# A hybrid attention and convolution layer step: first tiles, row sums, cache copies, turn and sample rows rearranged

## The chip, the cores and the metric

The kernel runs on one core of a Trainium2 chip. TensorE (PE in the rows, PEld for its weight loads) multiplies matrices, VectorE (DVE), ScalarE (ACT) and GpSimd (POOL) work on tiles, and SyncE (SP) issues every transfer into one queue that 16 DMA engines serve. The metric is the device time of one execution in microseconds (us). TensorE's clock is granted at one of two levels, 1.2 or 2.4 GHz; the profile shows the grant as a share, 0.5 or 1.0.

## What is computed

One layer for 512 prompt positions and 8 samples of 4 new tokens each, in fp32. The reference, cut:

```
h = rms_norm(x, norm_pre);  z = h @ w_in            # 2048 -> 60 column tiles of 128
q, k, v, g_att, c_a, c_b, g_conv = split(z)
att = attend(q, k, v)         # 12 heads; windows (128,1), (512,4), (2048,16), merged
u = c_a * sigmoid(c_b);  c = silu(layer_norm(depthwise_conv(u_pad)))
c = c @ conv_pw_w + conv_pw_b
mix = concat(att * silu(g_att), c * silu(g_conv))
y = mix @ w_out;  out = x + rms_norm(y, norm_post)
new_kv_sample = concat(cache_kv, k and v of the new tokens)[4:]   # per sample
```

The samples attend over a cache of 2048 rows of 12 KB for each of the 8 samples, and the last line is an output too: 2044 rows of each sample's cache come out again, moved up by four.

## The kernel before

Tokens are columns: 512 prompt tokens and 32 sample tokens, 544 in all, in two halves of 272. Products in fp32 are made of three fp32r matmuls: each operand is split into a rounded high part and the rest (`xh`, `xl` for x; `wh`, `wl` for weights; `mh`, `ml` and `owh`, `owl` in the output projection), and high*high, low*high and high*low are added in PSUM. ScalarE casts the high part, VectorE or GpSimd subtracts.

**First stage.** `project(n, ...)` makes one column tile of w_in: 16 rows of k, two halves, three matmuls, so 96 matmuls of 272 columns. The weights of a tile come in four loads of 256 KB (`load_w`, six buffers, five loads ahead) and are split on ScalarE (L800) and GpSimd (L801). For the first tile (n = 0) x itself arrives and is split (`split_x`, L250 and L251), and the sums of squares for the RMS norm are built along the way: a square of every x tile, and adds on VectorE and GpSimd (L257 to L261). `make_R` then turns the two partial sums into a factor for each token: ten pairs of matmuls `rqx`, a short chain on ScalarE and VectorE, diagonal tiles, matmuls `rbx`, and two copies into `R` (L302). No tile can leave PSUM before R is there. `make_tabs` (bias tables, matmuls `tb` and `rb`) runs in steps between the parts of tiles 1 and 2. From n = 3 on the samples' work runs beside the tiles.

**Order.** All engines' programs are held in the order in which the code is written (`in_order`). `tick()` counts quarter tiles; side jobs (heads, samples, convolution) are generators advanced at ticks. `bulk` copies cache rows from DRAM to DRAM whenever the bytes sent so far are under START + PACE * (columns that TensorE has been given): 8 MB + 159.5 bytes a column. `dma` issues all of it on SP, in order.

**Cache.** The samples' units (24 for K, 24 for V) load `kvf` (rows that are 16 apart, 0.75 MB, three buffers) and `kvm` (the last 512 rows, 1 MB, two buffers). What has been loaded is also written to the output from there (`store_far`, `store_mid`); the other rows go DRAM to DRAM, in 96 pieces of 1152 KB. In the V units the products `o` use four column groups of TensorE: four matmuls with 32 stationary columns each, one behind the other (`tile_position`, L106).

**Turn.** After tile 59, ScalarE and VectorE split all 16 tiles of the gated mix (`mh`, `ml`) and the samples' columns of them (`smix`), then the first w_out tiles. **Output projection.** Four column blocks c of 512; for each the row blocks (0, 1) and then (2, 3) of 128 tokens and the 32 sample rows, block 4. A step is one of 16 k rows: three matmuls of 512 columns for a prompt block, two for the samples (`smix` holds high and low side by side). In the last c the order is (0, 1), (2, 4), (3). `take_out` squares and scales, `finish` norms, adds x (`load_xt`) and stores.

Of the kernel before, what the change touches and what calls it, by code (L numbers as in the profile page):

```python
# [18 lines left out]
P = 128  # L19
D = 2048  # L20
# [17 lines left out]
TW = 640  # L38
PATTERNS = ((128, 1), (512, 4), (2048, 16))
# [5 lines left out]
START, PACE = 8_000_000, 159.5  # L45
# [37 lines left out]
def body(tc, xT, xtok, gpost, w_in, w_out, ckv, cconv, relb, vecs, pww, c_oht, c_ohr, c_lmr, c_tm, c_pick,  # L83
# [44 lines left out]
    last_w = [1 << 30]  # L128
# [16 lines left out]
    KORD = list(range(0, 8)) + list(range(12, 16)) + list(range(8, 12))  # L145

    def load_w(m):


        if m >= 4 * NTILE + NOUT or m in raws or m > last_w[0]:  # L150
            return
        n, qt = divmod(m, 4)
        raw = wpool.tile([P, 4, P], F32, tag="raw", name=f"raw{m}", bufs=6)
        if n < N_IN:
            dma(raw, w_in[order[n], qt])
        else:
            c, i = divmod(m - 4 * NTILE, KT)
            dma(raw.rearrange("p a b -> p (a b)"), w_out[c, KORD[i]])
        raws[m] = raw
# [25 lines left out]
    STARTS = (0, P, 2 * P, 3 * P, TOK - P)  # L185

    def token_rsqrt(sums, pool, name):


        ps = bank("q", f"rq{name}")  # L190
        for j, st in enumerate(STARTS):
            for i, ss in enumerate(sums):
                mm(ps[:, j:j + 1], ss[:, st:st + P], ones[:, 0:1], start=(i == 0), stop=(i == len(sums) - 1))
        r, v, w = [pool.tile([P, 5], F32, name=f"{n}{name}") for n in "rvw"]
        diag = pool.tile([P, 5, P], F32, name=f"diag{name}")
        nc.scalar.activation(r, ps[:, 0:5], AF.Sqrt, bias=epsc[:, 0:1], scale=1.0)
        nc.vector.tensor_scalar(v, ps[:, 0:5], EPS, None, op0=ALU.add)
# [4 lines left out]
        nc.vector.tensor_tensor(r, r, w, op=ALU.mult)  # L202
        out = []
        for hf, (j0, j1) in enumerate(((0, 3), (2, 5))):
            ps = bank("st"[hf], f"rb{name}{hf}")
            for j in range(j0, j1):
                if hf == 0 or j > 2:
                    nc.vector.tensor_scalar(diag[:, j, :], ident, r[:, j:j + 1], 2048.0, op0=ALU.mult, op1=ALU.mult)
                t0, t1 = max(j * P, hf * HT), min(j * P + P, hf * HT + HT)
                d0 = t0 - STARTS[j]  # L210
                mm(ps[:, t0 - hf * HT:t1 - hf * HT], ones, diag[:, j, d0:d0 + t1 - t0], start=True, stop=True)
            out.append(ps)
# [16 lines left out]
    rs_n = []  # L229
    ap_ = ExitStack()  # L230
# [4 lines left out]
    ssum = [ip.tile([P, TOK], F32, name=f"ssum{i}") for i in range(2)]  # L235

    def load_x(c):
        xr = ip.tile([P, 2, TOK], F32, tag="xr", name=f"xr{c}", bufs=6)
        dma(xr, xT[:, 2 * c:2 * c + 2, :])
# [4 lines left out]
    def split_x(c):  # L244
        xr = xrs.pop(c)
        for j in range(2):
# [8 lines left out]
            sq = ssum[k] if k < 2 else ip.tile([P, TOK], F32, tag="sq", name=f"sq{k}", bufs=3)  # L255
# [44 lines left out]
    def make_R():  # L300
        for hf, ps in enumerate(token_rsqrt(ssum, ip, "x")):
# [3 lines left out]
    d2d = [(b, a0, s0) for b in range(NB) for a0 in range(0, 96, 16) for s0 in (0, 6)]  # L305
    d2d_at = [0]

    def bulk(upto):
        while d2d_at[0] < len(d2d) and sent[0] < upto:
            b, a0, s0 = d2d[d2d_at[0]]  # L310
            d2d_at[0] += 1
            s = ckv[b].rearrange("(a s) c -> a (s c)", s=16)[a0:a0 + 16, (4 + s0) * ROW:(10 + s0) * ROW]
            o = o_kvs[b].rearrange("(a s) c -> a (s c)", s=16)[a0:a0 + 16, s0 * ROW:(6 + s0) * ROW]
# [3 lines left out]
    mixg = [keep.tile([P, 4, TOK], F32, name=f"mix{i}") for i in range(4)]  # L317
# [201 lines left out]
    def load_far(u):  # L519
# [4 lines left out]
        far = state["sp"].tile([P, 3, 512], F32, tag="kvf", name=f"kvf{u}", bufs=3)  # L524
# [13 lines left out]

    def store_far(u):
        g, kv, b = units[u]  # L540
        far = fars[u]
        off = (kv * NH + g * G4) * P
        dst = o_kvs[b, 0:NFAR, off:off + 512].rearrange("(a s) c -> a s c", s=16)
        dma(dst[15:31, 12:16, :], far[64:128, 0, :])
        dma(dst[0:15, 12:16, :], far[4:64, 0, :])
        dma(dst[31:63, 12:16, :], far[:, 1, :])
        dma(dst[63:95, 12:16, :], far[:, 2, :])

    def store_mid(u):
        g, kv, b = units[u]  # L550
        off = (kv * NH + g * G4) * P
        dma(o_kvs[b, NFAR - NT:PAST - NT, off:off + 512].rearrange("(j p) c -> p j c", j=4), mids[u])
# [17 lines left out]
    def k_phase(g, before):  # L570
# [53 lines left out]
        for b in range(NB):  # L624
# [10 lines left out]
            store_far(u)  # L635
# [12 lines left out]
            store_mid(u)  # L648
# [56 lines left out]
    def v_phase(g):  # L705
# [22 lines left out]
        for half in range(2):  # L728
            o = bank("acc", f"o{g}_{half}")
            for s in range(4):  # L730
# [5 lines left out]
                store_far(u)  # L736
# [3 lines left out]
                for j in range(8):  # L740
# [11 lines left out]
                    if j == 2:  # L752
# [5 lines left out]
                        store_mid(u)  # L758
# [24 lines left out]

    def add(gen, delay, rank):
# [4 lines left out]
    AHEAD = 5  # L789

    def split(ci):
        if ci >= 4 * NTILE or ci in splits:
            return
        for a in range(AHEAD + 1):
            load_w(ci + a)
        raw = raws.pop(ci)
        raws[ci] = None
# [396 lines left out]
```

## Time and profile before

| | |
|---|---|
| time, median of 3 runs | 1212.15 us (1211.03 to 1212.73) |
| the profiled execution | 1209.32 us, its span 1207.5 us |
| PE busy | 1158.5 us, 96% of the span |
| DVE, ACT, POOL busy | 686.3, 374.1, 419.9 us |
| DMA | 397.52 MB, the queue's packets fill 93.8% of 16 engines' span |
| mean granted clock | 0.98 |

How to read the rows below. A line of a stage table gives a stretch in us from the span's start, its length, then for PE, PEld, DVE, ACT and POOL the busy us with the number of instructions, the mean granted clock, the mean share of the 16 DMA engines that was busy and the GB/s that they moved. A line of the timeline gives start, length, engine, line of the code, operation, output and inputs, shape, and in brackets how long the engine had been idle and what ended that. In a row of PE, one fp32 matmul has two records; a fp32r matmul has one. PE spans are those of pipelined matmuls, so the rate is read from start to start. A DMA row gives the number of issues, the size and the median us from issue to landing.

### The profile page before, as it was taken

Reading aid. Unit: us, or ns where it says so; the run is one execution under the profiler, and the core shown is the slowest. Engines: PE = TensorE matmul, PEld = TensorE weight load, DVE = VectorE, ACT = ScalarE, POOL = GpSimd, SP = SyncE. Lnnn points to the kernel's source line nnn. Section 1 sums busy time; section 2 is a strip of 40 time slices with the busy share of each in tenths; the row PEclk is TensorE's granted clock in tenths of the full one; section 3 lists DMA queues with packets and bytes.
Section 4 is the critical chain, followed back from the end, with each engine's and each line's share of the span. In section 5 each row is a group of like instructions: output and inputs, shape, how many; then the busy total and the mean of one; then the engine's idle time right before and its main releaser. Section 6 shows DMA issues by size and latency. Waiting matters only on the chain.

```text
span 1207.5 us, 24127 instructions
## 1 busy us (share of the span) xinstructions
PE 1158.5 (96%) x9342; PEld 1063.2 (88%) x9342; DVE 686.3 (57%) x2015; ACT 374.1 (31%) x759; POOL 419.9 (35%) x357
## 2 busy tenths in 40 slices
PE   5899999999999999999999999999999959999995
PEld 4799999999899999999999999999999948888884
DVE  7306989789889988777332676982221161202125
ACT  6223333322122432331343333322212162214121
POOL 5244333343334332343233222433433442314120
PEclk8799999999999999999999999999999979999998
DMA  9599999999999999999999999989999949899997
GB/s 340 200 367 360 345 328 348 341 287 348 310 330 333 344 345 343 385 366 312 335 357 350 357 350 336 317 311 393 330 325 347 348 159 330 317 328 347 329 338 229
DMA packets 161255, 397.52 MB, mean 329 GB/s; under 512 B 20007, under 2 KB 22823, under 8 KB 157940
## 3 DMA queue, kind: packets, MB, share of 16 engines
q1 hardware_dynamic: 161140, 395.98, 93.8%
q8 instruction: 73, 1.20, 0.4%
q14 instruction: 42, 0.34, 0.1%
HBM read 296.51 MB, written 212.66 MB: 422 GB/s over the span
## 4 chain that ended last, share of the span: by engine, by line
PE 46%; DMA 6%; issue 4%; DVE 3%; POOL 1%; ACT 1%; SPq 0%; DVEq 0%; POOLq 0%; ACTq 0%
PE z L104 26%; PE oz L104 13%; PE o L106 3%; DMA xt<-in_xtok_dram 3%; DMA kvf<-in_ckv_dram 1%; DMA toep<-dtab 1%; DVE qsc L631 1%; PE att L104 1%; DMA raw<-in_w_out_dram 1%; PE s L104 1%; POOL wl L801 1%; PE pwp L104 1%; DVE y L1038 0%; SPq L95 0%; PE t L110 0%
## 5 line engine op out<-in xcount | busy, mean ns | idle before, releaser
L104 PE MATMUL z<-xh,wh 128*128 128x272 f32 x1920 | 575.9, 300 | 6.6 <-ACT xh L250 6.6
L104 PE MATMUL z<-xl,wh 128*128 128x272 f32 x1920 | 557.7, 290 | 9.7 <-DVE xl L251 9.6
L104 PE MATMUL z<-xh,wl 128*128 128x272 f32 x1920 | 557.3, 290 | 0.0
L801 POOL TENSOR_TENSOR wl<-raw,wh 128x512 fp32r<-128x512 f32 x240 | 329.4, 1381 | 477.0 <-ACT wh L800 422.5
L104 PEld LDWEIGHTS z<-xh,wh 128*128 128x128 f32 x1920 | 366.1, 191 | 22.4 <-issue 12.0
L104 PEld LDWEIGHTS z<-xl,wh 128*128 128x128 f32 x1920 | 365.5, 190 | 14.6 <-DVE xl L251 12.5
L104 PEld LDWEIGHTS z<-xh,wl 128*128 128x128 f32 x1920 | 365.7, 190 | 0.0
L800 ACT CAST wh<-raw 128x512 fp32r<-128x512 f32 x240 | 146.7, 617 | 198.5 <-PE z L104 124.3
L322 DVE TENSOR_TENSOR t<-z,R 128x272 f32<-128x272 f32 x96 | 42.0, 438 | 186.2 <-PE z L104 173.7
L631 DVE SCALAR_TENSOR_TENSOR qsc<-kvf,qb 128x128 f32<-128x128 f32 x288 | 126.6, 440 | 8.8
L631 DVE SCALAR_TENSOR_TENSOR qsc<-kvm,qb 128x128 f32<-128x128 f32 x288 | 111.3, 387 | 9.3 <-DMA kvm<-in_ckv_dram 0.6
L104 PE MATMUL oz<-owh,mh 128*128 128x512 f32 x256 | 102.5, 400 | 13.9 <-ACT owh L827 13.9
L828 POOL TENSOR_TENSOR owl<-raw,owh 128x512 fp32r<-128x512 f32 x43 | 61.8, 1464 | 125.9 <-ACT owh L827 96.8
L104 PE MATMUL oz<-owl,mh 128*128 128x512 f32 x256 | 102.1, 399 | 0.3 <-POOL owl L828 0.3
L430 DVE SCALAR_TENSOR_TENSOR mix<-up,vec,mix 128x512 f32<-128x512 f32 x120 | 102.2, 852 | 0.0
L104 PE MATMUL oz<-owh,ml 128*128 128x512 f32 x256 | 102.1, 399 | 0.0
L104 PEld LDWEIGHTS oz<-owh,mh 128*128 128x128 f32 x256 | 48.7, 190 | 25.5 <-ACT owh L827 14.1
L827 ACT CAST owh<-raw 128x512 fp32r<-128x512 f32 x64 | 37.6, 618 | 86.9 <-DMA raw<-in_w_out_dram 79.0
L432 DVE SCALAR_TENSOR_TENSOR mix<-us,vec,mix 128x32 f32<-128x32 f32 x120 | 61.9, 516 | 0.0
L1021 DVE TENSOR_TENSOR y<-oz,gp 128x512 f32<-128x512 f32 x16 | 11.1, 691 | 87.4 <-ACT osq L1020 87.1
L104 PEld LDWEIGHTS oz<-owl,mh 128*128 128x128 f32 x256 | 48.9, 191 | 12.7 <-POOL owl L828 1.1
L104 PEld LDWEIGHTS oz<-owh,ml 128*128 128x128 f32 x256 | 48.8, 190 | 11.5
(185 smaller groups left out, 1063.1 us busy)
## 6 DMA issues: line engine op xcount, KB each, us to landing
out_dram<-in_ckv_dram SPq DMA_DIRECT2D x96, 1152.0 KB, 9.9
raw<-in_w_in_dram SPq DMA_DIRECT2D x240, 256.0 KB, 6.9
kvm<-in_ckv_dram SPq DMA_DIRECT2D x48, 1024.0 KB, 8.7
out_dram<-kvm SPq DMA_DIRECT2D x48, 1024.0 KB, 10.5
kvf<-in_ckv_dram SPq DMA_DIRECT2D x144, 256.0 KB, 8.6
out_dram<-kvf SPq DMA_DIRECT2D x96, 256.0 KB, 4.5
raw<-in_w_out_dram SPq DMA_DIRECT2D x64, 256.0 KB, 6.5
out_dram<-kvf SPq DMA_DIRECT2D x48, 128.0 KB, 7.6
```

Of the source, the lines that this page charges most:

```text
L104: nc.tensor.matmul(out, lhsT, rhs, start=start, stop=stop)
L106: nc.tensor.matmul(out, lhsT, rhs, start=start, stop=stop, tile_position=tile_position)
L322: nc.vector.tensor_tensor(dst[:, sl], z[hf][:, :HT], R[:, sl], op=ALU.mult)
L430: nc.vector.scalar_tensor_tensor(cc[:, ct, :SEQ], up[:, j:j + SEQ], wj, cc[:, ct, :SEQ], op0=ALU.mult, op1=ALU.add)
L432: nc.vector.scalar_tensor_tensor(cs, us[:, :, j:j + NT], wj, cs, op0=ALU.mult, op1=ALU.add)
L631: nc.vector.scalar_tensor_tensor(scr, src[:, hh * P:hh * P + P], SCALE, qb[:, hh * P:hh * P + P], op0=ALU.mult, op1=ALU.mult, accum_out=sd ...
L800: nc.scalar.copy(wh, raw)
L801: nc.gpsimd.tensor_tensor(wl, raw, wh.bitcast(F32), op=ALU.subtract)
L827: nc.scalar.copy(wh, raw)
L828: (nc.vector if j % 3 == 2 else nc.gpsimd).tensor_tensor(wl, raw, wh.bitcast(F32), op=ALU.subtract)
L1021: nc.vector.tensor_tensor(ys[b][:np_, cs], z[:np_, :], gp[:np_, cs], op=ALU.mult)
```

## The change

The first three tiles are made side by side in six PSUM banks (`project_first`): k rows outermost, so each x tile, when it has been split, feeds three tiles. Of the last four k rows the second half stands behind `make_R`. The sums of squares no longer come from the columns of x: x is loaded a second time by tokens (`load_xtok`, five tiles of up to 1 MB, into the buffers of the mix), and ScalarE squares and sums each tile in one instruction (`square`). `make_tabs` stands between these tiles and n = 3. Weight loads become 512 KB in four buffers. `store_far` and `store_mid` are gone, and all 2044 cache rows of a sample go DRAM to DRAM, 176 pieces of mostly 1152 KB; `kvf` has two buffers. START and PACE become 4 MB and 166.3. Before the turn, two mix tiles, most of the samples' columns and four w_out tiles are prepared early. The samples' output rows leave the 128-wide steps: `sample_rows` does four k rows at once in four column groups, in fp32 with the unsplit weights `oraws`, and `take_out` adds the four groups. In the last c the blocks are (0, 1), (2), (3), and x for them is loaded in 512 KB pieces.

```diff
-START, PACE = 8_000_000, 159.5
+START, PACE = 4_000_000, 166.3
...
-        raw = wpool.tile([P, 4, P], F32, tag="raw", name=f"raw{m}", bufs=6)
+            raw = wpool.tile([P, 8, P], F32, tag="raw", name=f"raw{m}", bufs=4)
...
-            if k % 4 == 1:
-                nc.vector.tensor_tensor(sq, xr[:, j, :], xr[:, j, :], op=ALU.mult)
-            else:
-                nc.scalar.activation(sq, xr[:, j, :], AF.Square)
-            if k >= 2:
-                (nc.vector if k % 2 else nc.gpsimd).tensor_tensor(ssum[k % 2], ssum[k % 2], sq, op=ALU.add)
+    def square(b):
+        t_ = xt_of(b)
+        nc.scalar.activation(t_, t_, AF.Square, accum_out=sumsq[:P if b < 4 else NS, b:b + 1])
...
-    d2d = [(b, a0, s0) for b in range(NB) for a0 in range(0, 96, 16) for s0 in (0, 6)]
+    d2d = [(b, r, min(96, PAST - NT - r)) for b in range(NB) for r in range(0, PAST - NT, 96)]
...
-        far = state["sp"].tile([P, 3, 512], F32, tag="kvf", name=f"kvf{u}", bufs=3)
+        far = state["sp"].tile([P, 3, 512], F32, tag="kvf", name=f"kvf{u}", bufs=2)
...
-            store_far(u)
...
-            store_mid(u)
...
+        ws = prepare(0)
+        for c in range(4):
+            nxt = prepare(c + 1) if c < 3 else None
+            if c == 2:
+                square(0)
+                load_xtok(4)
+                square(1)
+            if c == 3:
+                for b in range(2, 5):
+                    square(b)
+            rows(c, ws, 0, 2)
+            if c < 3:
+                rows(c, ws, 2, 4)
+            ws_, ws = ws, nxt
+        make_R()
+        rows(3, ws_, 2, 4)
+        for n in range(NF):
+            for hf in range(2):
+                outs[n](hf, z[n])
...
+            if n == NF - 1:
+                project_first(first)
+                add(make_tabs(), 0, 0)
+                now[0] += 8
+                for _ in range(4):
+                    tick()
...
+        if n == N_IN - 3:
+            smix = ring["a"].tile([P, KT, NS], F32, name="smix")
+            for g in (0, 1, 3):
+                nc.gpsimd.tensor_copy(smix[:, 4 * g:4 * g + 4, :], mixg[g][:, :, SEQ:])
+            for i in range(NPRE):
+                split_mix(i)
...
+    def sample_rows():
+        while due:
+            j0 = due.pop(0)
+            c = j0 // KT
+            if c not in sz:
+                sz[c] = bank("acc", f"os{c}")
+            for a in range(4):
+                i = (j0 + a) % KT
+                mm(sz[c][a * NS:a * NS + NS, :], smix[:, KORD[i], :], oraws.pop(j0 + a).rearrange("p a b -> p (a b)"),
+                   start=(i < 4), stop=(i >= KT - 4), tile_position=(0, a * NS))
+            if (j0 + 4) % KT == 0:
+                take_out(c, 4, sz[c])
...
-                    if b == 4:
-                        mm(z_, smix[:, i, :], wh, start=(i == 0), stop=False)
-                        mm(z_, smix[:, i, :], wl, start=False, stop=(i == KT - 1))
```

Three places in the order. The first is ScalarE between the last x tile and the first weights of the next stage (`xh` and `wh` are splits, `rx` the root for R, `R` its copies, `tabs` and `base` the tables). Before:

```order
L800 CAST wh_352<-raw_127 128x512
L196 ACT_TABLE_LOAD
L196 ACTIVATE rx<-rqx,epsc 128x5
L302 COPY R<-rbx_402 128x272
L302 COPY R<-rbx_409 128x272
L800 CAST wh_423<-raw_143 128x512
L800 CAST wh_429<-raw_173 128x512
L287 COPY tabs<-tb 12x512
L287 COPY tabs<-tb 12x128
L800 CAST wh_467<-raw_233 128x512
```

And after, where the `mix` rows are the squares of x by tokens:

```order
L273 ACTIVATE mix_87,sumsq<-mix_87 128x2048
L273 ACTIVATE mix_88,sumsq<-mix_88 128x2048
L273 ACTIVATE mix_89,sumsq<-mix_89 128x2048
L273 ACTIVATE mix_86,sumsq<-mix_86 128x2048
L273 ACTIVATE mix_87,sumsq<-mix_87 32x2048
L200 ACTIVATE rx<-sumsq,epsc 128x5
L314 COPY R<-rbx_546 128x272
L314 COPY R<-rbx_550 128x272
L299 COPY tabs<-tb 12x512
L299 COPY tabs<-tb 12x128
L309 COPY base<-rb 96x512
L309 COPY base<-rb 96x416
```

The five squares stand right behind the last two `xh`, and the first weight cast of tile 3, `wh_632`, is the row behind the last `base`; before, weight casts stood between all of these.

The second place is ScalarE at the turn, from the last `th` (of the last gate) on. Before:

```order
L942 ACTIVATE th_11984<-t_11868 128x544
L984 CAST mh_11998<-mix_99 128x544
L986 CAST smix<-mix_99 128x32
L984 CAST mh_12004<-mix_99 128x544
L986 CAST smix<-mix_99 128x32
```

Fourteen more such pairs follow, and then the first cast of w_out, `owh_12104`. After:

```order
L843 CAST owh_11550<-raw_11370 128x512
L843 CAST owh_11554<-raw_11370 128x512
L843 CAST owh_11560<-raw_11438 128x512
L843 CAST owh_11564<-raw_11438 128x512
L1039 ACTIVATE th_11570<-t_11437 128x544
L786 CAST mh_11585<-mix_86 128x544
L786 CAST mh_11589<-mix_86 128x544
```

Twelve more mh follow, and then `owh_11656`, the fifth cast of w_out. What moved: four owh from behind all mh to ahead of th, and two mh and all smix casts out of this stretch.

The third place is TensorE in the output projection. Before, in a step of blocks 2, 3 and 4:

```order
L104 MATMUL oz_3_12303<-owh_12104,mh_11998 128x512
L104 MATMUL oz_3_12303<-owh_12104,ml_11999 128x512
L104 MATMUL oz_3_12303<-owl_12105,mh_11998 128x512
L104 MATMUL oz_4_12304<-owh_12104,smix 128x512
L104 MATMUL oz_4_12304<-owl_12105,smix 128x512
```

After, at the start of c = 0, behind the last z of tile 59:

```order
L107 MATMUL z_1_11473<-xh_412,wl_11470 128x272
L109 MATMUL os_11647<-raw_11370,smix 32x512 x2
L109 MATMUL os_11647<-raw_11438,smix 32x512 x2
L107 MATMUL oz_0_11652<-owh_11550,mh_11295 128x512
L107 MATMUL oz_0_11652<-owh_11550,ml_11296 128x512
L107 MATMUL oz_0_11652<-owl_11551,mh_11295 128x512
```

`os` is the samples' bank. The two sample matmuls of each step became one matmul of 32 stationary columns for each k row, four in a row, and they read the loaded weights `raw` themselves, so a buffer of `raw` is free only when TensorE has passed them.

## Rows read from the trace of the kernel before

**Rows 1.** The page: the DMA queue, and traffic at the DRAM.

```profile
q1 hardware_dynamic: 161140, 395.98, 93.8%
HBM read 296.51 MB, written 212.66 MB: 422 GB/s over the span
```

**Rows 2.** Stage tables of stretches of the span, columns as explained under the profile.

```profile
6.50:30.00 23.50, 15.58 (x59) 13.17 (x60) 22.73 (x20) 16.34 (x28) 16.02 (x9) 0.85 1.01 376
...
40.00:76.40 36.40, 33.95 (x233) 31.73 (x232) 4.55 (x19) 8.65 (x17) 12.19 (x11) 0.90 0.70 248
76.40:968.90 892.50, 889.22 (x8120) 840.45 (x8119) 578.03 (x1830) 275.41 (x559) 322.67 (x284) 1.00 0.98 342
...
968.90:982.80 13.90, 0.01 (x1) 0.02 (x1) 12.88 (x33) 11.98 (x35) 1.68 (x2) 0.62 0.30 108
982.80:990.20 7.40, 7.07 (x17) 5.14 (x18) 4.71 (x7) 4.39 (x8) 7.39 (x5) 0.55 0.46 122
990.20:1194.80 204.60, 204.58 (x880) 165.03 (x878) 49.38 (x84) 50.04 (x103) 54.44 (x39) 1.00 0.93 322
1000.00:1160.00 160.00, 160.00 (x689) 129.33 (x688) 27.82 (x34) 39.78 (x81) 45.64 (x33) 1.00 0.96 339
1194.80:1207.50 12.70, 0.00 (x0) 0.00 (x0) 6.41 (x15) 0.98 (x3) 0.00 (x0) 0.61 0.59 186
```

**Rows 3.** Timeline of the start, one engine each: PE, ACT and DVE.

```profile
21.18 0.59 PE L104 MATMUL z<-xl,wh 128*128 128x272 f32 x1 [3.53 <-DVE xl L251]
...
42.51 0.27 ACT L196 ACTIVATE rx<-rqx,epsc 128x5 f32<-128x5 f32 x1 [8.40 <-PE rqx L104]
...
47.06 0.39 ACT L302 COPY R<-rbx 128x272 f32<-128x272 f32 x1 [0.92 <-PE rbx L104]
...
53.48 0.39 PE L104 MATMUL tb<-oht,rel 33*12 33x128 f32 x2 [0.67 <-ACT tabs L287]
...
76.67 0.41 DVE L915 TENSOR_TENSOR mix<-z,R 128x240 f32<-128x240 f32 x1 [2.55 <-PE z L104]
```

**Rows 4.** Chain of waits, in order of time: start us, us, what.

```profile
478.98 0.86 PE s L104 x2
...
544.22 0.79 PE o L106 x24
545.02 6.25 PE z L104 x48
```

**Rows 5.** Timeline of PE: two matmuls of a tile, eight apart.

```profile
545.18 0.29 PE L104 MATMUL z<-xl,wh 128*128 128x272 f32 x1
...
546.19 0.29 PE L104 MATMUL z<-xh,wh 128*128 128x272 f32 x1
```

**Rows 6.** Timeline of the turn: ACT, PE and POOL.

```profile
969.39 0.66 ACT L942 ACTIVATE th<-t 128x544 f32<-128x544 f32 x1 [10.33 <-DVE t L322]
...
973.46 0.64 ACT L984 CAST mh<-mix 128x544 fp32r<-128x544 f32 x1
...
982.78 0.79 PE L104 MATMUL oz<-owh,mh 128*128 128x512 f32 x1 [13.90 <-ACT owh L827]
...
982.81 12.41 POOL L828 TENSOR_TENSOR owl<-raw,owh 128x512 fp32r<-128x512 f32 x8 [9.82 <-ACT owh L827]
```

**Rows 7.** Timeline of the end: SP and DVE.

```profile
1197.07 1.88 SPq L95 DMA_DIRECT2D xt<-in_xtok_dram  x4
...
1202.95 1.41 DVE L1038 SCALAR_TENSOR_TENSOR y<-y,stat,xt 128x512 f32<-128x512 f32 x2 [0.51 <-DMA xt<-in_xtok_dram]
```

**Rows 8.** DMA issues, 1000 to 1160 us: count, KB each, median us to landing.

```profile
out_dram<-in_ckv_dram SPq DMA_DIRECT2D x38, 1152.0 KB, 16.1
raw<-in_w_out_dram SPq DMA_DIRECT2D x44, 256.0 KB, 10.6
xt<-in_xtok_dram SPq DMA_DIRECT2D x4, 256.0 KB, 15.8
```

More of the change, by code (lines that the diff above doesn't have):

```diff
@@ L38 @@
 TW = 640
+_KORD = list(range(0, 8)) + list(range(12, 16)) + list(range(8, 12))
 PATTERNS = ((128, 1), (512, 4), (2048, 16))
@@ L183, in body, with token_rsqrt @@
     nc.vector.memset(ones, 1.0 / 2048)
[L185 to L197, printed above, removed]
+    sumsq = keep.tile([P, 5], F32, name="sumsq")
+    nc.vector.memset(sumsq, 1.0)
+    def token_rsqrt(ss, pool):
+        r, v, w = [pool.tile([P, 5], F32, name=n + "x") for n in "rvw"]
+        diag = pool.tile([P, 5, P], F32, name="diagx")
+        nc.scalar.activation(r, ss, AF.Sqrt, bias=epsc[:, 0:1], scale=1.0 / 2048)
+        nc.vector.tensor_scalar(v, ss, 1.0 / 2048, EPS, op0=ALU.mult, op1=ALU.add)
         nc.vector.reciprocal(r, r)
@@ L229, in body @@
     rs_n = []
+    mixg = [keep.tile([P, 4, TOK], F32, name=f"mix{i}") for i in range(4)]
     ap_ = ExitStack()
@@ L877, in samples @@
             state["vdone"] = g
+    nc.scalar.activation(sumsq[:, 0:1], epsc, AF.Sqrt)
     load_w(0)
-    for c in range(8):
-        xrs[c] = load_x(c)
-        if c % 2:
-            load_w(1 + c // 2)
-    bulk(START)
+    xrs[0] = load_x(0)
+    load_w(2)
+    load_w(4)
+    xrs[1] = load_x(1)
+    dma(raws[0][:, 4:8, :], w_in[order[0], 0][:, 4:8, :])
+    xrs[2] = load_x(2)
+    xrs[3] = load_x(3)
+    for n in range(NF):
+        load_w(2 * n + 1)
+        xrs[4 + n] = load_x(4 + n)
+    xrs[7] = load_x(7)
+    for b in range(4):
+        load_xtok(b)
+    load_w(2 * NF)
+    load_w(2 * NF + 1)
     load_tabs()
+    first = []
     for n in range(N_IN):
@@ L904, in body, with out @@
             t_ = apool.tile([P, TOK], F32, tag=nm, name=f"t{n}", bufs=2 if nm == "k" else 1)
-        def out(hf, z):
-            if n == 0 and hf == 0:
-                make_R()
+        def out(hf, z, t_=t_, c=c, g=g if c < 3 * NH else None, hh=hh if c < 3 * NH else None, nm=nm, n=n):
+            if n == N_IN - 1 and hf == 0:
+                for j in range(4):
+                    split_out(j)
             if c >= NH:
@@ L1013, in take_out @@
         if b == 4:
-            low = op.tile([NS, 512], F32, name=f"low{c}", tag="low")
-            nc.scalar.copy(low, z[NS:2 * NS, :])
-            nc.vector.tensor_tensor(low, z[0:NS, :], low, op=ALU.add)
-            z = low
-        sq = op.tile([P, 512], F32, name=f"osq{c}_{b}", tag="osq")
+            part = z[0:NS, :]
+            for i in range(1, 4):
+                low = op.tile([P, 512], F32, name=f"low{c}_{i}", tag="low", bufs=2)[:NS, :]
+                nc.scalar.copy(low, z[NS * i:NS * i + NS, :])
+                nc.vector.tensor_tensor(low, part, low, op=ALU.add)
+                part = low
+            z = part
+        sq = op.tile([P, 512], F32, name=f"osq{c}_{b}", tag="low", bufs=2)
         nc.scalar.activation(sq[:np_, :], z[:np_, :], AF.Square, accum_out=stat[:np_, b, c:c + 1])
```

261 lines of the change are left out of this document (149 added, 112 removed).

## The prediction

> **What bounds the kernel now.** I read four views in this order: the page's queue line, the stage tables, the timelines of the places where TensorE stands still, and the chain of waits for prices. The stage tables [rows 2] cut the span into four. From 76.4 to 968.9 us TensorE is busy for 889.2 of 892.5 us at the full granted clock, 2.4 GHz: it is the bound, and nothing can be won there without fewer columns. In the same stretch, though, the 16 DMA engines are busy at a share of 0.98: a second bound stands a few per cent behind the first. The queue as a whole is filled for 93.8% of the span [rows 1]. What is exposed are the edges. Before 76.4, TensorE does three tiles (n = 0 to 2) that would need 36 us; that tile 3 starts there is seen by VectorE's last read of tile 2 at 76.67 [rows 3]. At the turn TensorE idles for 13.9 us, released by a w_out cast on ScalarE [rows 6], and then needs 7.4 us for 17 matmuls at a clock of 0.55 [rows 2], the lower level. After the last matmul 12.7 us remain. So three edges, 880 matmuls of the output stage, and a nearly full queue are what a change can touch.
>
> **Prices.** Eight prompt matmuls of 272 columns lie between 545.18 and 546.19 [rows 5]: 0.126 us each, a tile of 96 is 12.1 us. The output stage makes 880 matmuls in 204.6 us [rows 2]: 0.2325 each. An fp32 matmul of 512 columns alone takes 0.86 us (its two records, [rows 4]); the 12 fp32 matmuls of 128 columns in four column groups take 0.79 us (24 records), 0.066 each, and the z behind them starts at 545.02, 0.01 after they end. All sums go against the profiled execution's own 1209.3 us; the median of the runs, 1212.15, lies 2.8 above it, which I add at the end.
>
> **The start (-16.4).** Side by side, TensorE needs 288 x 0.126 = 36.3 us for the three tiles and is fed three times as much per x tile, so the 3.5 us waits for `xl` as at 21.18 [rows 3] go. What is late next is R. In ScalarE's order the five squares stand behind all x splits, and x by tokens comes behind x by columns and three tiles' weights in the queue: about 12 MB, at the start's 376 GB/s [rows 2] 32 us, so its last big tile lands near 38 to 41. A square of 2048 columns is not in the trace: from 0.39 for 272 columns [rows 3] and 0.64 for 544 [rows 6], 2.0 to 2.9 us. By ScalarE alone (last x split at about 31, five squares) and by the queue (last big tile, its square, and the small fifth one, whose buffer is free only after the first square) the root begins at about 43, as it does now (42.51). From there to the last R copy took 47.06 + 0.39 - 42.51 = 4.9 us [rows 3], so R stands at 48, against tile 3's need for it at the end of the side-by-side stretch. TensorE has by then done 252 of its 288 matmuls and waits; the last 36 take 36 x 0.126 = 4.5 us at full clock, 8 at half. Then `make_tabs` stands alone: four matmuls, four copies of up to 512 columns on ScalarE, about 4 x (0.5 + 0.64) = 4.6 us, with waits like the 0.67 at 53.48 [rows 3]; now it stands between matmuls of tiles 1 and 2 and is hidden. Behind it the first weight cast (0.64) and its `wl` on GpSimd (12.41 / 8 = 1.55 us, [rows 6]). That puts tile 3 at 58, and some 2 us of low clock behind the waits make it worth 60. From 76.4: -16.4; 56 to 64 are the ends (squares at 2.0 and full clock; queue late and low clock). SP itself waits for the first square before it can issue the fifth x load, and the first cache pieces, the table store `dtab` (which waits for `tabs`) and tile 4's weights are queued behind that; tile 4 is needed 12 us after tile 3, so I cost this at nothing.
>
> **The turn (-9.5).** Now ScalarE does `th` (0.66), sixteen `mh` (0.64) with a `smix` each and the first `owh` before TensorE has anything: 13.9 us idle, and the 7.4 us behind it are worth 3.7 at full clock: 17.6 lost. After, `th` still waits for the last tile, but four `owh` stand ahead of it and two `mh` are done: TensorE has the first samples' group (about 0.95) and steps 0 and 1 at once, and steps 2 and 3 as their `mh` come. A step of six matmuls is 6 x 0.2325 = 1.4. Step 4 waits for the fifth `owh`, behind th and 14 `mh`: 0.7 + 14 x 0.66 + 0.6 = 10.5, and 1.55 for `owl`: 12 us. By then TensorE has 0.95 x 2 + 4 x 1.4 = 7.5 us of work: 4.5 idle and up to 3.7 of low clock, 8 in all. 17.6 - 8.1 = 9.5; ends 6 (more low clock, since the waits are scattered) and 14.
>
> **The samples' rows (-14.6).** 2 of the 14 matmuls of every k row go: 4 x 16 x 2 = 128, at 0.2325 that is 29.8 us, all on the path. Added are 64 fp32 matmuls of 512 columns in 16 groups of four. In column groups: 64 x 4 x 0.066 = 16.9 us; if four run in the time of one: 16 x 0.86 = 13.7. Both rows are near, I take 15.2. There are 32 switches between the groups and full-width matmuls; the row shows 0.01 us at one, so I add nothing. The Trainium skill, "TensorEngine Tiling (Array Packing)", Key Properties, says that changing the tiling mode drains TensorE; it gives no figure, the row with its 0.01 us does not bear a cost out, and by either the sum stays as it is. The extra adds in `take_out` are on VectorE, busy for 49 of 204.6 us there [rows 2].
>
> **The end (-3.3).** Of the 12.7 us, x for the last block is issued at 1197.07 behind stores, and the last y waits for it until 1202.95 [rows 7]. With x loaded earlier some 3.3 us of this go; ends 0 and -4.
>
> **The queue (+5).** The cache rows no longer come from what was loaded, but the bytes through the queue are the same, apart from 4.5 MB more x; only their places differ. Counting loads, stores and cache pieces by the code's own rule, tiles 3 to 59 carried 303 MB (340 GB/s by this count, where the row has 342) and now carry 316, 136 of the 176 cache pieces sent by then; the first 123 us of the output stage then carry 45 MB with the other 40. What the queue can do: 342 / 0.98 = 349 GB/s with the present mix, 339 / 0.96 = 353 where DRAM to DRAM dominates, 376 where only loads run [rows 2]. Half cache pieces and half larger loads: between 353 and 376. 316 MB at 355 is 890 us, no longer than TensorE needs; 45 MB at 353 is 127.5, 4.5 over. With little slack, waits of single tiles remain: I take +5, with ends 0 (376) and +19.6 (349: 13.6 and 6).
>
> **Sum.** -16.4 - 9.5 - 14.6 - 3.3 + 5 = -38.8, so 1170.5 on the profiled execution's basis, 1173 for the median.
>
> **The rivals.**
> *The queue is the bound.* At 349 GB/s the z stage takes 906 us and the output stage 6 more: 1188; at the 342 that flowed, 316 / 342 = 924 and 9 more: 1209. For it: the share of 0.98, and 0.96 with 339. Against it: packets get larger and fewer. Seen as gaps before z with a weight or kvf wait.
> *More of it.* All edges at their good ends and no toll: 1156.
> *Weights late in the output stage (the other side).* A `raw` buffer of w_out used to be free when the casts had read it, now only when the samples' matmuls have passed it. Four buffers of 512 KB hold 16 k rows, so a reload has about 8 steps of 1.4 = 11.2 us, and a w_out load lands in 10.6 us now, a cache piece in 16.1, x in 15.8 [rows 8]. If loads of double size take 16, TensorE waits 4.9 us twice in each of four column blocks, 39 us, and with 3.7 of low clock behind each wait 69: around 1225. With the low clock it decides from 13.0 us to landing (8 x 5.5 = 44). Against it: the cache pieces end in the third block, and a landing time in a full queue is mostly the queue ahead.
> *It doesn't do what it says: the groups run one by one.* 64 x 0.86 = 55 us in place of 15.2: 1213, no change, or more with low clock. Against it: [rows 4], 3 to 4 at a time.
> *Traffic at the DRAM.* A cache piece is read again: 296.5 + 80 x 1.1 + 4.5 = 389 MB read and 213 written, 602 MB [rows 1]. If the 422 GB/s of now were a ceiling, 1426 us; it decides below 602 / 1.212 = 497. Against it: from 1000 to 1160 us 54.2 MB flowed, 44.8 of them in 38 cache pieces [rows 2, 8] that count twice: 619 GB/s. The Trainium skill, "HBM Reference", Specifications, puts an effective 358 GB/s to a core; taken for reads and writes together, 602 MB would need 1680 us. The 422 already measured disagrees, and I give it no more than this rival's chance.
>
> **How the numbers follow.** About 0.2% (2.4 us) is what a measurement of this kernel can tell from no change. Forecast, 1161 to 1184: 0.64. More of it: 0.08. Queue the bound, 1184 to 1209: 0.18. Weights late: 0.04. Groups one by one: 0.04. DRAM: 0.02. Slower: most of weights late 0.03, half of the groups' 0.02, DRAM 0.02: 0.07. Same: the rest of these and the queue's far end: 0.05. Faster: 0.88. The range 1156 to 1200 takes in the good ends and the queue at 349, and leaves out the far queue and the slower rivals, under 0.2.
>
> **What would show it.** Start: VectorE's last read of tile 3 at about 72 us, the first z of tile 3 at 58 to 60, ScalarE at squares just before R. Turn: idle of TensorE ending with the fifth `owh` or its `owl`, 4 to 5 us in place of 13.9. Samples: 16 groups of about 0.95 us, without a gap behind. End: under 10 us behind the last matmul. Queue: a share near 1.0 at 353 GB/s or more in the z stage with TensorE's gaps under 1%; gaps of several us before z there would make the prediction wrong, as would w_out loads that land after more than 13 us.

## The result

The changed kernel took 1173.74 us (median of 4 runs, 1170.97 to 1174.14) where the kernel before took 1212.44 on the same chip: a ratio of 0.968, 95% interval 0.966 to 0.970, 38.7 us faster. The forecast was 1173, in a range of 1156 to 1200. The profiled execution took 1170.97, its span 1169.2, against 1209.32 and 1207.5 before: 38.3 us between the spans.

The stage table of the changed kernel, with the columns of [rows 2]:

```profile
6.50:42.40 35.90, 34.16 (x252) 33.71 (x252) 16.76 (x16) 24.61 (x36) 17.95 (x13) 1.00 0.96 370
42.40:59.40 17.00, 10.93 (x57) 6.71 (x56) 4.87 (x21) 5.12 (x11) 0.00 (x0) 0.86 0.74 245
59.40:953.50 894.10, 891.18 (x8118) 842.24 (x8118) 579.27 (x1831) 279.71 (x567) 328.99 (x292) 1.00 0.97 355
953.50:961.50 8.00, 8.00 (x41) 4.67 (x40) 7.00 (x12) 7.39 (x14) 1.46 (x2) 1.00 0.50 166
961.50:968.20 6.70, 1.52 (x5) 0.98 (x5) 6.61 (x10) 5.28 (x10) 5.18 (x2) 0.83 0.47 155
968.20:974.00 5.80, 5.80 (x21) 2.89 (x20) 1.42 (x1) 1.14 (x2) 5.52 (x5) 0.61 0.67 196
974.00:1160.00 186.00, 185.79 (x835) 138.22 (x833) 52.86 (x92) 51.42 (x106) 46.97 (x35) 1.00 0.91 327
1160.00:1169.20 9.20, 0.14 (x1) 0.00 (x0) 4.44 (x12) 0.98 (x3) 0.00 (x0) 0.71 0.36 135
```

Four differences of boundaries make the 38.3 us. Tile 3 starts at 59.4 in place of 76.4: -17.0. The z stage is 894.1 us long in place of 892.5: +1.6. From its end to the last matmul 206.5 in place of 225.9: -19.4. The end 9.2 in place of 12.7: -3.5. The page's lines on the queue and the DRAM, as [rows 1]:

```profile
q1 hardware_dynamic: 95972, 400.42, 93.6%
HBM read 388.65 MB, written 212.66 MB: 514 GB/s over the span
```

Packets fell from 161 to 96 thousand, and the DRAM carries 601 MB in place of 509 MB, at 514 GB/s.

The start, timelines of ScalarE and of TensorE (start us, us, engine, line, operation, and in brackets the idle time and what ended it):

```profile
41.98 1.91 ACT L273 ACTIVATE mix<-mix 32x2048 f32<-32x2048 f32 x1 [3.47 <-DMA mix<-in_xtok_dram]
44.01 0.30 ACT L200 ACTIVATE rx<-sumsq,epsc 128x5 f32<-128x5 f32 x1
...
45.79 1.52 PE L107 MATMUL rbx<-diagx,ones 128*128 128x128 f32 x12 [3.30 <-DVE diagx L208]
...
53.50 0.39 PE L107 MATMUL tb<-oht,rel 33*12 33x128 f32 x2 [0.66 <-ACT tabs L299]
...
59.42 0.60 PE L107 MATMUL z<-xh,wh 128*128 128x272 f32 x1 [1.11 <-ACT wh L809]
```

R is late, as foreseen, but not for the four big squares: ScalarE stood idle for 3.47 us until the fifth x tile, 32 tokens, had landed. Its load stands on SP behind the table constants. Then the tables run alone to 59.4, TensorE busy for 4.8 of 7.6 us at a clock of 0.68. The turn, on TensorE, and a group of the samples' matmuls with what stands around it:

```profile
962.99 0.50 PE L107 MATMUL oz<-owh,mh 128*128 128x512 f32 x1 [1.48 <-ACT owh L843]
...
967.42 0.80 PE L107 MATMUL oz<-owl,mh 128*128 128x512 f32 x1 [3.70 <-POOL owl L844]
...
1013.13 0.40 PE L107 MATMUL oz<-owl,mh 128*128 128x512 f32 x1
1013.45 1.06 PE L109 MATMUL os<-raw,smix 128*32 128x512 f32 x8
1014.45 0.50 PE L107 MATMUL oz<-owh,mh 128*128 128x512 f32 x1
1014.79 0.40 PE L107 MATMUL oz<-owh,ml 128*128 128x512 f32 x1
1015.02 0.39 PE L107 MATMUL oz<-owl,mh 128*128 128x512 f32 x1
```

At the turn TensorE idles for 1.48 + 3.70 = 5.2 us, against 13.9 in [rows 6], and 5.8 us at a clock of 0.61 follow. The chain of waits has the `owl` that TensorE waited 3.70 us for:

```profile
963.02 4.36 POOL owl L844
```

It is one subtraction on GpSimd, which takes 1.28 us at the median of the three before the turn (947.2 to 949.7). Here VectorE ran `ml` beside it, one behind the other, up to 965.6. A group of four sample matmuls takes 1.00 us from start to start. But the matmul ahead of it takes 0.32 and the one behind 0.34, where 0.23 is the pace of the others: each switch between a group and the 128-wide matmuls costs about 0.1 us.

### The profile page after: what moved, and what is told of

Read it like the earlier page. It is cut to its first block, busy times and chain, and to the rows that moved or that the text cites. A ratio compares the mean times of both kernels' runs of the same rounds, so it can differ in the third digit from the quotient of the medians.

```text
span 1169.2 us, 23598 instructions
## 1 busy us (share of the span) xinstructions
PE 1137.5 (97%) x9322; PEld 1029.4 (88%) x9322; DVE 674.0 (58%) x1997; ACT 378.1 (32%) x749; POOL 406.8 (35%) x353
## 4 chain that ended last, share of the span: by engine, by line
PE 56%; DVE 2%; DMA 1%; issue 1%; POOL 0%; ACT 0%; SPq 0%; DVEq 0%; ACTq 0%; POOLq 0%
PE z L107 32%; PE oz L107 14%; PE o L109 3%; PE pwp L107 1%; PE os L109 1%; PE att L107 1%; DMA raw<-in_w_out_dram 1%; PE s L107 1%; PE t L113 1%; DVE qsc L628 1%; POOL owl L844 0%; PE kt L113 0%; PE pvar L107 0%; PE pm L107 0%; PE sn L109 0%
## 5 line engine op out<-in xcount | busy, mean ns | idle before, releaser
L810 POOL TENSOR_TENSOR wl<-raw,wh 128x512 fp32r<-128x512 f32 x228 | 311.1, 1374 | 471.3 <-ACT wh L809 447.7
L809 ACT CAST wh<-raw 128x512 fp32r<-128x512 f32 x228 | 139.1, 617 | 181.4 <-PE z L107 106.4
L442 DVE SCALAR_TENSOR_TENSOR mix<-up,vec,mix 128x512 f32<-128x512 f32 x120 | 107.6, 896 | 0.0
L844 POOL TENSOR_TENSOR owl<-raw,owh 128x512 fp32r<-128x512 f32 x43 | 61.4, 1447 | 111.2 <-ACT owh L843 81.8
L844 DVE TENSOR_TENSOR owl<-raw,owh 128x512 fp32r<-128x512 f32 x21 | 21.7, 1032 | 73.0 <-ACT owh L843 72.8
L444 DVE SCALAR_TENSOR_TENSOR mix<-us,vec,mix 128x32 f32<-128x32 f32 x120 | 57.0, 475 | 0.0
## 6 DMA issues: line engine op xcount, KB each, us to landing
out_dram<-in_ckv_dram SPq DMA_DIRECT2D x168, 1152.0 KB, 12.2
kvm<-in_ckv_dram SPq DMA_DIRECT2D x48, 1024.0 KB, 10.5
```

Of the source, the lines that this page charges most:

```text
L442: nc.vector.scalar_tensor_tensor(cc[:, ct, :SEQ], up[:, j:j + SEQ], wj, cc[:, ct, :SEQ], op0=ALU.mult, op1=ALU.add)
L444: nc.vector.scalar_tensor_tensor(cs, us[:, :, j:j + NT], wj, cs, op0=ALU.mult, op1=ALU.add)
L809: nc.scalar.copy(wh, raw)
L810: nc.gpsimd.tensor_tensor(wl, raw, wh.bitcast(F32), op=ALU.subtract)
L844: (nc.vector if j % 3 == 2 else nc.gpsimd).tensor_tensor(wl, raw, wh.bitcast(F32), op=ALU.subtract)
```

## The experiments

Two theories stood against each other. **T**: TensorE bounds all of the z stage, and the gain is what the sum said, edge by edge (start, turn, samples' rows, end). **Q**: the DMA queue, with a share of 0.97 and 0.98, is the bound or nearly so, so that the new cache copies and packets made the room, or what is won elsewhere is given back. All runs but the repetition are the changed kernel with something altered. The kernel before took 1203.6 to 1212.4 us in the five sets of runs, the changed kernel 1173.7 and 1174.7 in two; variants are therefore compared with 1174 us in time, and differences under 2 us are not read. The ratios in the expectations start from 0.968, the ratio to a kernel before of 1212 us; in the sets where it took 1207 the changed kernel's 1174 is a ratio of 0.973.

**The changed kernel again.**

> The changed kernel unaltered, on the chip of these runs, since the kernel before took 1212 us on one chip and 1206 to 1207 on two others. Theory T (TensorE bounds the changed kernel, the queue bounded the kernel before a little): 1171 to 1175 whatever the chip, and a ratio that moves with the time of the kernel before. Rival (one chip is faster in all): ratio 0.968 again, 1167 to 1169 where the kernel before takes 1207.

1174.7 us (1172.5 to 1175.4), with 1210.1 for the kernel before and a ratio of 0.970 (0.968 to 0.972). The time stays, the ratio moves with the kernel before: T holds, on the one other chip that was tried. Why the kernel before varies by 9 us between sets was not tried.

**The samples' rows in one column group.**

```diff
-                mm(sz[c][a * NS:a * NS + NS, :], smix[:, KORD[i], :], oraws.pop(j0 + a)...,
-                   start=(i < 4), stop=(i >= KT - 4), tile_position=(0, a * NS))
+                mm(sz[c][0:NS, :], smix[:, KORD[i], :], oraws.pop(j0 + a)...,
+                   start=(i == 0), stop=(i == KT - 1), tile_position=(0, 0))
```

> The changed kernel, but all 64 fp32 matmuls of the samples' rows in one column group, accumulating in one place (the three adds of take_out go). Theory T (four groups run side by side, 0.99 us for four): one by one 64 x 0.86 = 55 us in place of 15.9, 1173.7 + 39 = 1213; a group of four about 3.4 us. Rival: 32 stationary columns cost less than 128 even alone, or the chip overlaps them anyway: 1174 to 1185, a group of four under 1.6 us.

1205.4 us, +31. The chain of waits has the group of four (eight records) so, first of this kernel, then of the changed one:

```profile
1021.56 3.55 PE os L109 x8
```

```profile
1020.31 0.99 PE os L109 x8
```

3.55 is four times 0.86 and a little: without the groups there is no overlap at all. 16 x 2.56 = 41 us would follow; from the last z to the last matmul the profile has 32 more (238.4 in place of 206.2). The changed kernel loses 8.1 us at the turn to idle time and low clock and 1.3 at one wait for raw (both worked out below); here the longer groups fill these, and the turn has one wait of 0.29 us. T holds, and a matmul at a wait costs less than its length.

**Early casts at the turn taken back.**

```diff
-            if n == N_IN - 1 and hf == 0:
-                for j in range(4):
-                    split_out(j)
...
     for i in range(NPRE, KT):
         split_mix(i)
+    for j in range(4):
+        split_out(j)
```

> The changed kernel with the first four casts of w_out behind all mh instead of ahead of the last th. Theory T (ScalarE's order sets TensorE's idle time at the turn): TensorE waits th + 14 mh + owh, 0.7 + 14 x 0.55 + 0.6, and owl 1.45 behind the last z, about 10 us less the samples' group, in place of 5.2, and low clock as before: 1179 to 1184. Rival (the turn got shorter because the samples' casts and two mh left ScalarE, not by the early owh; waits later go down by as much): 1173 to 1176.

1180.8 us (1179.0 to 1182.1), +7. TensorE's waits at the turn:

```profile
964.51 0.80 PE L107 MATMUL oz<-owh,mh 128*128 128x512 f32 x1 [8.39 <-ACT owh L843]
...
969.54 0.79 PE L107 MATMUL oz<-owl,mh 128*128 128x512 f32 x1 [3.81 <-POOL owl L844]
```

12.2 us of idle time in place of 5.2: seven more, and seven in the time. The place of the four casts is worth that; T holds.

**One tile while x arrives.**

```diff
-NF = 3
+NF = 1
```

(The first loads and the place at which the samples' work begins follow from it.)

> The changed kernel with one tile in place of three while x arrives; tiles 1 and 2 follow one by one, R still by tokens, tables between tiles 0 and 1. Theory T (the start's gain is the work of tiles 1 and 2 done before R is there, 24 us less what R gains from 2 MB less in the queue ahead of x): R some 5 us earlier, the first z of tile 3 at 71 to 77 us in place of 59.4, 1185 to 1192. Rival (the gain comes from the shorter way to R, squares by tokens): 1172 to 1179.

1189.5 us (1189.3 to 1191.8), +15. TensorE, ScalarE (the fifth square, and the root for R), and VectorE's last read of tile 2:

```profile
39.24 2.77 PE L107 MATMUL rbx<-diagx,ones 128*128 128x128 f32 x12 [16.95 <-DVE diagx L208]
...
35.43 1.91 ACT L273 ACTIVATE mix<-mix 32x2048 f32<-32x2048 f32 x1 [5.24 <-DMA mix<-in_xtok_dram]
37.47 0.30 ACT L200 ACTIVATE rx<-sumsq,epsc 128x5 f32<-128x5 f32 x1
...
81.33 0.41 DVE L997 TENSOR_TENSOR mix<-z,R 128x240 f32<-128x240 f32 x1 [2.55 <-PE z L107]
```

`rx` at 37.5 is 6.5 us earlier than in the changed kernel, and 5.0 earlier than the 42.51 of the kernel before [rows 3]. So the squares by tokens do not make R late by themselves: with one tile first, and fewer cache copies at the start, it comes sooner than it did by columns. Still tile 3 starts at about 81.3, behind even the 76.4 of the kernel before: TensorE waits 17 us for R with nothing to do, its clock is 0.50 up to 53.8 and 0.81 from there to 70, and the tables stand alone, 9.0 us from 44.8 to 53.8. The side-by-side tiles gain by filling the wait. T holds, a little stronger than put (71 to 77). A kernel with one tile first and hidden tables, or with three tiles and the squares by columns, was not run, so what the squares by tokens give by themselves stays open.

**Cache rows stored from SBUF again.** The edit is the diff of `store_far`, `store_mid` and `d2d` in the change, read backwards. With `kvf` in three buffers, as in the kernel before, the samples' tiles need 50.4 KB of a partition where 46.75 are left; that form has no time, and `kvf` has two here.

> The changed kernel with one part undone: cache rows that have been loaded are stored from SBUF again, and 96 pieces go DRAM to DRAM; kvf stays at two buffers (three don't fit), so a kvf buffer is now free only when its four stores have landed. Theory T (TensorE bounds the z stage, the queue has slack either way): ratio to the kernel before within 0.004 of the 0.968 of the changed kernel, tile 3 to the last z within 3 us of 895. Rival Q (the new way through the queue, 96 thousand packets in place of 161 thousand, keeps the z stage free): 316 MB at 342 to 349 GB/s, 11 to 30 us more, ratio 0.977 to 0.993. Second rival (two buffers of kvf, not the rate, hold the samples up): TensorE or VectorE wait for kvf by name, with the DMA share under 0.95.

1174.3 us (1174.1 to 1175.7): no difference. (The ratio of 0.973 lies outside T's words by the kernel before, 1207.0 in that set.) Tile 3 to the last z is 894.2 us long, and in it TensorE's waits for kvf or its stores are 1.0 us together (0.5 in the changed kernel), so the second rival is out as well. 139 thousand packets; the same stretch of the z stage is shown with the next two.

**No cache copies; more of them a column; fewer.** The first drops the one line that issues the copies, the others set PACE.

> The changed kernel without its 176 DRAM-to-DRAM pieces (it leaves out 2044 cache rows of each sample; their bytes still count in the program's own pace). Theory T (the queue is just covered, nearly no toll is left): 0 to 4 us less than the changed kernel, ratio 0.9645 to 0.968. Rival Q (the queue is the bound in some stretch): 8 us less or more, ratio under 0.961, TensorE's idle time down in the z or the output stage.

> The changed kernel with PACE 180 in place of 166.3: cache pieces are sent 8% faster a column, 27 MB more by the end of the z stage, 387 GB/s asked for there. Theory T (the second bound lies at 367 to 374 GB/s, as the densest stretch of the changed kernel shows with a share of 0.98): TensorE is held up in the z stage until the pieces run out, 15 to 35 us more than the changed kernel. Rival (only few per cent are lost, since the program's own order spreads the waits): under 8 us more.

> The changed kernel with PACE 150: 32 MB fewer by the end of the z stage, some 27 cache pieces more in the output stage. Theory T (in the output stage a raw buffer is free 8 steps, 11.2 us, ahead of its use, and w_out lands in 9 to 11.6 us now, just under that): pieces ahead of w_out in the queue make the landing longer than 13 us, TensorE waits for raw there, 15 to 45 us more than the changed kernel, with the z stage unchanged. Rival (the pieces are sent behind the weights at the end, bytes alone count): 72 MB in 206 us are under 353 GB/s, 0 to 5 us more.

Without copies 1173.0 us (1170.2 to 1174.7), -1, not to be told from none. With PACE 180 1180.2 us, +6; with PACE 150 1272.9 us, +99. The stretch 76 to 950 us of the changed kernel, then of the kernel with stores from SBUF, of the one without copies, and of PACE 180, with 120 to 240 us of the last:

```profile
76.00:950.00 874.00, 871.62 (x7984) 823.13 (x7984) 577.88 (x1827) 275.31 (x559) 318.97 (x284) 1.00 0.97 356
```

```profile
76.00:950.00 874.00, 871.73 (x7986) 823.24 (x7985) 578.45 (x1829) 276.68 (x562) 317.99 (x284) 1.00 0.99 357
```

```profile
76.00:950.00 874.00, 871.72 (x7985) 823.23 (x7984) 578.50 (x1829) 277.17 (x562) 316.81 (x283) 1.00 0.55 180
```

```profile
76.00:950.00 874.00, 871.09 (x7980) 822.53 (x7979) 577.07 (x1828) 276.02 (x561) 318.46 (x285) 1.00 1.01 386
120.00:240.00 120.00, 120.00 (x980) 114.00 (x979) 98.65 (x371) 45.73 (x104) 42.50 (x42) 1.00 1.02 399
```

TensorE is busy for 871.6 us of the stretch at a share of 0.97, for 871.7 at 0.55 and for 871.1 at 1.01. Halving what the queue carries wins nothing, and 8% more costs half a microsecond there. Q falls for the z stage, and so do T's own 367 to 374 GB/s: the queue moved 399 GB/s over 120 us without holding TensorE up. A share of 0.97 was not a bound 3% away. From the last z to the last matmul, too, it takes 206.3 us without the copies and 206.2 with them.

With PACE 180 that stretch is 4.0 us longer, most of the 6. There w_out comes through a longer queue: `os` waits for raw four times, 6.3 us together, twice at the turn (1.9, where the idle time for `owh` and `owl` falls from 5.2 to 1.4) and twice in the output stage (4.4). Two rows of its chain of waits in the output stage, a load of w_out and the matmuls that it released:

```profile
996.97 24.07 DMA raw<-in_w_out_dram
1021.08 1.68 PE os L109 x4
```

The load landed after 24.1 us, behind nine cache pieces issued from 977.7 on. From 990 to 1021 us the queue moved 317 to 334 GB/s at a share of 0.96 to 1.01. So a load that is needed at once can still be held up by what was sent ahead of it.

Both expectations on PACE 150 were wrong. The z stage is unchanged, w_out lands in 5.2 us, TensorE's last matmul starts at 1160.9. But the copies are paced by TensorE's columns, and what is left goes out in one heap near the end. SyncE:

```profile
1163.45 80.78 SPq L98 DMA_DIRECT2D out_dram<-in_ckv_dram  x29
1246.70 10.62 SPq L98 DMA_DIRECT2D out_dram<-y  x4
```

29 pieces, 33 MB, run with TensorE finished, and the last rows of y wait behind them in the one queue. So the copies are free at 166.3; at 150 the list isn't empty when TensorE ends, and at 180 pieces stand in front of w_out.

**The start: the fifth x tile and the tables earlier.**

```diff
                 square(0)
                 load_xtok(4)
+                load_tabs()
                 square(1)
...
         make_R()
-        rows(3, ws_, 2, 4)
+        split(4 * NF)
+        t = make_tabs()
+        next(t)
+        rows(3, ws_, 2, 4, (0,))
+        next(t)
+        rows(3, ws_, 2, 4, (1,))
+        next(t)
+        rows(3, ws_, 2, 4, (2,))
...
-    load_tabs()
...
-                add(make_tabs(), 0, 0)
```

> The changed kernel with two steps of its start moved: the fifth x tile by tokens is issued ahead of the small constant loads, and the four steps of the tables stand between the last matmuls of tiles 0 to 2, with tile 3's first weight cast ahead of them. Theory T (the start is set by R, which waited 3.5 us for that x tile, and by the tables, 7 us of ScalarE and TensorE in turns): R about 3.5 us earlier, first z of tile 3 at 49 to 53 in place of 59.4, 6 to 10 us less than the changed kernel, ratio 0.960 to 0.963. Rival Q (what is won at the start is given back in the z stage, since the queue has no slack): tile 3 earlier, but the ratio 0.966 to 0.968.

1165.1 us (1162.6 to 1166.5), -9. ScalarE's wait for that tile, and TensorE at tile 4:

```profile
38.79 1.92 ACT L273 ACTIVATE mix<-mix 32x2048 f32<-32x2048 f32 x1 [0.28 <-DMA mix<-in_xtok_dram]
...
71.61 0.39 PE L107 MATMUL z<-xh,wh 128*128 128x272 f32 x1 [1.23 <-ACT wh L809]
72.96 0.39 PE L107 MATMUL z<-xh,wl 128*128 128x272 f32 x1 [0.83 <-POOL wl L810]
```

The 3.5 us wait is 0.3. VectorE first reads tile 3 at 61.4, where the changed kernel does at 71.7: ten earlier, of which a new wait, tile 4's weights behind the cache pieces on SP, takes 2.1 back. T holds; what Q says is seen only there, as an order on SP and not as a rate.

**The turn: casts woven among the mh.**

```diff
+    sample_rows()
     for i in range(NPRE, KT):
         split_mix(i)
+        if 4 <= i < 8:
+            split_out(i)
```

> The changed kernel with the fifth to eighth cast of w_out standing between the mh of the turn, and the first group of samples' matmuls ahead of them in the order of the program. Theory T (ScalarE's order sets the idle time of the turn): casts come at 1.1 us a step, TensorE takes 1.4, so its 5.2 us of idle time and some 3 us of low clock go: 5 to 8 us less than the changed kernel, ratio 0.961 to 0.964. Rival (the weights' rest on GpSimd, or raw's landing, is next): idle time down by under 2 us, ratio 0.966 to 0.968.

1172.2 us (1170.8 to 1176.8), -2: the rival. TensorE no longer waits for a cast but for a load:

```profile
966.67 3.18 PE L109 MATMUL os<-raw,smix 128*32 128x512 f32 x8 [2.67 <-DMA raw<-in_w_out_dram]
```

Its idle time there is 3.5 us in place of 5.2. k rows 8 to 11 need a raw buffer that is free only when the samples' first group has passed it, at the end of tile 59.

**Both, with the samples' first group in the middle of tile 59.** The first four casts and the first `sample_rows()` move into `project` ahead of tile 59's third quarter, and the loads of k rows 8 to 11 behind them; the start is that of the run with x and tables early, with tile 4's second load ahead of the table store. Then the same with casts woven up to the eleventh k row, the samples' second group placed among them, and:

```diff
-        (nc.vector if j % 3 == 2 else nc.gpsimd).tensor_tensor(wl, raw, ...)
+        (nc.vector if j % 3 == 2 and j >= KT else nc.gpsimd).tensor_tensor(wl, raw, ...)
```

> The changed kernel with the start of the run with x and tables early (and tile 4's second weight load issued ahead of the table store), and with the turn woven, where the first group of samples' matmuls and the first four w_out casts stand in the middle of tile 59 and the loads of k rows 8 to 11 are issued behind that group. Theory T (with the casts woven, the turn waited for raw's landing, because a raw buffer is free only when the samples' matmuls have passed): 8 us from the start and 5 to 8 from the turn, 13 to 17 us less than the changed kernel on the same chip, 1157 to 1161. Rival Q (the queue gives part of it back): 1162 to 1167, with waits for raw at the start or the turn.

> The run with start and turn changed, but the casts of w_out woven up to the eleventh k row, and in the first column block all the weights' rests (owl) on GpSimd, none on VectorE behind the ml. Theory T (in that run the turn waited 7.9 us for an owl of VectorE that stood behind 14 ml, each of them 1.2 us beside a busy GpSimd in place of 0.65): that wait and some 2 us of low clock go, 8 to 10 us less, 1156 to 1159, TensorE's idle time at the turn under 2 us. Rival (GpSimd at 1.45 us a step is as slow as TensorE's 1.4, or raw's landing is next): idle time of 3 us or more is left, 1161 to 1166.

The first took 1165.6 us (1165.1 to 1169.4), no better than the start alone. The time is the rival's, the cause neither's. TensorE at the turn, and VectorE:

```profile
969.90 0.79 PE L107 MATMUL oz<-owl,mh 128*128 128x512 f32 x1 [7.93 <-DVE owl L844]
...
957.44 11.81 DVE L787 TENSOR_TENSOR ml<-mix,mh 128x544 fp32r<-128x544 f32 x10
```

The wait went on to VectorE: an `owl` behind ten `ml`, which take 1.18 us each on the mean. The second took 1158.4 us (1156.9 to 1161.5), a ratio of 0.963 (0.961 to 0.965) to a kernel before that took 1203.6 in that set; in time 15 to 16 us less than the changed kernel. Its turn:

```profile
950.00:970.00 20.00, 20.00 (x93) 14.04 (x91) 20.00 (x13) 12.49 (x24) 20.00 (x13) 1.00 0.74 271
```

TensorE is busy through all of it at full clock; one wait for raw, 1.9 us at 1001, is left in the output stage. Three things had been late in turn: ScalarE's order, the load behind the buffer, VectorE's order. Several edits stand together in this run, and what each gives in it was not taken apart.

## Why the prediction was right, and where it was not

The time and each place were right; the terms less so, and two errors met, by luck.

- **Start.** Forecast 16.4 with the low clock in it; measured 17.0 less the 1.6 by which the z stage grew, its first 16.6 us at a clock of 0.84: 15.4. `rx` began at 44.0 (forecast 43), a square took 1.90 (2.0 to 2.9). That the 43 came near is partly luck, since what made it late was mis-named: the fourth big square began without a wait at 36.5, before the 38 to 41 at which its tile was to land, and then a load of 256 KB behind small constants on SP cost 3.47 us, not squares or bandwidth. The tables and the cast behind them took 7.6 us (from 51.8 to 59.42), where I had 4.6 and 0.64: 2.8 of it are waits, which I left out, and the matmuls ran at a clock of 0.68.
- **Turn.** Forecast 8.1 us lost; measured 8.1. From the end of the last z to 974.1 (20.7 us) TensorE did 39 prompt matmuls at 0.232 and three groups at 1.19, switches included, which need 12.6; of the rest 5.2 are idle time, the others mostly low clock. Before, 13.9 of idle time and 7.4 less 17 x 0.2325 make 17.4. Gain 9.3 in place of 9.5. Inside it two terms were off: the fifth `owh` came 9.5 us after the last z (forecast 10.5), and its `owl`, put at 1.55 as if GpSimd were alone, took 4.36 beside VectorE's `ml`.
- **Samples' rows.** Forecast 15.2 us; a group is 0.99, near the upper bound of 1.05, and the switches, costed at nothing by one row, are 0.2 us a group: 19.0 us. Gain 10.8 in place of 14.6: this term was mis-sized by 3.8. The Trainium skill, "TensorEngine Tiling (Array Packing)", Key Properties, has changing the mode drain TensorE: the 0.1 us at each switch agree with a small cost of that kind, though no run tells a drain from a weight load or from the change between fp32r and fp32. With all samples' rows in one column group, still 32 wide, the switches cost the same (0.33 ahead, 0.34 behind). That row, 0.01 us in [rows 4], was the chain's bookkeeping of ends; the starts of the kernel before show it, 0.23 from the first z behind `o` to the next one at 545.18 [rows 5], where 0.126 is the pace:

```profile
544.95 0.39 PE L104 MATMUL z<-xh,wh 128*128 128x272 f32 x1
```

- **End.** Forecast 3.3, measured 3.5.
- **Queue.** Forecast +5; measured one wait of `os` for raw, 0.2 us of idle time, 1.3 from start to start (the two halves of that group take 1.26 and 0.99 in place of 0.50 each). The step that failed is the capacity, read as GB/s over busy share (349 to 376 GB/s). In the z stage the experiments put it at 399 or more; in the output stage of PACE 180 a load was late at 317 to 334, so one figure for the queue doesn't hold at all. So the rival with 0.18 had hardly a chance, and the one on the DRAM, 422 as a ceiling, falls by 514 over the span.

-15.4 - 9.3 - 10.8 - 3.5 + 1.3 = -37.7; the prompt's 768 matmuls, at 0.2319 from start to start (704 of them from 974 to 1160 us) in place of 0.2325, are another -0.5, and -38.2 stands against -38.3. The samples' 3.8 too much and the queue's 3.7 too much cancelled: a size in the one, the capacity in the other. Weights late in the output stage came near: a landing of 11.6 us gave that wait, and with PACE 180 the rival came true for one load. (Its 1225 takes the 69 us from the good ends, 1156; from the 1168 of the other rivals it is 1237.)

## To carry to other kernels

When several tiles are made side by side so that a late factor finds TensorE busy, the work in front of the factor and behind it (a small load in the wrong place of the queue, a table on two engines in turns) is what is left to win: here 9 us by order alone. At the hand-over between the stages one engine after the other was the late one here; weave all of them step by step, look at buffers that are freed by the engine that waits, and at VectorE and GpSimd working side by side. A DMA share near 1 said here that the queue was kept filled, not that it was full: run the kernel with the copies left out and with more of them before costing a toll. And take costs from start to start: ends of matmuls are modelled, and idle time between them showed 0.2 us where 1.3 were lost.

## What the runs showed of the hardware

- The same queue moved 342 to 357 GB/s at a share of 0.97 to 0.99, 386 to 399 at 1.01 to 1.02, and 317 at 1.01 in the output stage of PACE 180 (990 to 1005 us): busy share and rate are not proportional.
- VectorE and GpSimd slowed each other. The 14 `ml` of the turn, all of one shape, in the changed kernel and then in the last run, where GpSimd is busy for 20.00 of 20 us (durations in ns: shortest, median, longest):

```profile
L787 DVE TENSOR_TENSOR ml<-mix,mh x14: 711/714/815, 956.6 to 964.9; 128x544 fp32r<-128x544 f32 x14
```

```profile
L787 DVE TENSOR_TENSOR ml<-mix,mh x14: 719/1808/1817, 949.7 to 970.1; 128x544 fp32r<-128x544 f32 x14
```

In the first, `ml` takes 0.71 us, and GpSimd's `owl` beside the last of them takes 4.36 in place of 1.28; in the second `ml` takes 1.81 and `owl` 1.77 at the median. In the run between them (both, first form) the four `ml` from 957.4 to 959.3, with GpSimd idle, took 0.71 and the next six, beside its `owl`, 1.78 at the median. Which of the two gives way, and when, was not tried. The Trainium skill, "GPSIMD Engine Reference", Specifications, has GpSimd share VectorE's SBUF interfaces, with contention for VectorE instructions of two SBUF inputs. `ml` and `owl` both have two, and these rows agree with it.
